# A bidirectional mLSTM and delta-rule layer on one core: when the decay loads, four modulation sums and the first z pieces are issued, and how the hand-over from output projection to FFN is cut

## The chip, the core and the metric

The kernel runs on one core of a Trainium2 chip. The metric is device time in microseconds (us) of one execution. The engines that matter are TensorE (PE, matrix products and transposes), VectorE (DVE), ScalarE (ACT), GpSimd (POOL, here it clears small tiles, scales a few blocks and issues small transfers) and SyncE (SP, it issues the weight loads).

## The reference

One layer on 256 tokens of width 2048, all in float32:

```python
mod = silu(c) @ ada_w + ada_b           # shift, scale, gate of the mixer and of the FFN
h = rms_norm(x) * (1 + scale_m) + shift_m
proj = h @ w_in                         # columns of branch A, branch B and the merge gates
y_a = (sigmoid(a_o) * norm(bidirectional(mlstm, q_a, k_a, v_a))) @ w_branch_a      # 4 heads
y_b = (norm(bidirectional(gated_delta, q_b, k_b, v_b)) * silu(b_z)) @ w_branch_b   # 16 heads
x = x + gate_m * ((g_a * y_a + g_b * y_b) @ w_out)
hf = rms_norm(x) * (1 + scale_f) + shift_f
gt, up = split(hf @ w_gate_up)          # 5632 columns each
x = x + gate_f * ((silu(gt) * up) @ w_down)
return rms_norm(x)
```

The gated delta rule works in chunks of 64 tokens; every chunk inverts a unit triangular matrix (`triangular_solve`), whose entries hold products of keys, beta and ratios of the decay.

## The kernel before

**Products in three parts.** A float32 weight block is loaded (`raw_*`, 1 MB), rounded on ScalarE to its high part (`wh_*`) and subtracted on VectorE to its low part (`wl_*`); the activations have a high and a low part too (`hh`/`hl`, later `mgh`/`mgl` and `hfh`/`hfl`). PE then multiplies high by high (L229), high weight by low activation (L230) and low weight by high activation (L231). `tjob` does this for 512 output columns and both halves of the tokens (`t`), in halves of a block: 12 matmuls of 512 columns for each `wh`/`wl` pair. There are three `raw` buffers and three of `wh` and of `wl`.

**Order.** Helper generators hand out pieces of such products ("jobs") between the steps of the recurrent branches, and `pump` adds from time to time one sum of the modulation (`ada_parts`, L111: a load of 1 MB and one VectorE instruction over 128x2048 that multiplies and accumulates). `every[0]` sets after how many job pieces a sum comes. The four engines' programs are otherwise put in order by a scheduler; instructions wrapped in `order(...)` keep the order of the code among themselves.

**Branch B.** Its 16 heads run in four groups. `gdn_phase1(h)` prepares a head: the decay factors `al` come from HBM, broadcast to all partitions (`decay_load`, 256 KB), four scans (L586 to L589) make `dec` of them, PE makes the key and query products `ks`, ten VectorE instructions (L633 to L642) and a transpose make the triangular blocks `mi` and `mb` (one buffer each). POOL stores `mi` to HBM in four transfers (`inst_d`, L649) and loads the blocks back into the layout of the inversion (`uu`, L652). `gdn_invert(g)` inverts the blocks of the group's four heads on VectorE, `gdn_phase2` applies them. `corners` copies blocks of `mi` and `mb` to `cc` on ScalarE; it is put off until the next `settle()`. Between two groups stands the job `z` (`z_job`, the output gate of the next group).

**Output projection and FFN.** `o` is made in four column blocks (`o0` to `o3`). For `o3` the last four row blocks are done first for token half 0 and then for token half 1 (`by_token`), so that the end of half 0 overlaps PE's work on half 1. For each half, `residual` multiplies by the gate (`tmss`, L1166), adds to `x` (L1167) and takes the sum of squares on ScalarE (L1170); `token_rstd` sums the four parts, takes the root and the reciprocal (L1178 to L1180). Then `normed` scales the token rows (`xn`), `moved` transposes a block of 128 features on PE (`pxn`), scales and shifts it (`hf`, L1264 or L1262), rounds it to `hfh` (L1265), and `low` makes `hfl` (L1268). The first FFN column block `gt0` runs beside that, in pairs of feature blocks. `d` (the down projection) ends like `o3`, with `finish` in place of the transposes.

Of the kernel before, what the change touches and what calls it, by code (L numbers as in the profile page):

```python
# [9 lines left out]
F32 = mybir.dt.float32  # L10
# [42 lines left out]
def hybrid_block(ctx: ExitStack, tc: tile.TileContext, xr, nfr, crow, pk_d, cst_d, ada2, ada4, win0, winb, wint, wba, wbb, wo, wgu, wd, out, dbg=None):  # L53
# [138 lines left out]
                done(o)  # L192
            yield True

    def tjob(name, chunks, xh, xl, done, early=0, by_token=None, steps=1):

        raws = {}  # L200

        def halves(u, k0):
            if u not in raws:
                raws[u] = raw_tile([P, 4, 512], f"raw_{name}_{u}")
                nc.sync.dma_start(raws[u], chunks[u])
            wh = st.tile([P, 2, 512], F32R, tag="wh", bufs=3, name=f"wh_{name}_{u}_{k0}")
            wl = st.tile([P, 2, 512], F32R, tag="wl", bufs=3, name=f"wl_{name}_{u}_{k0}")
            order(S.activation(wh, raws[u][:, k0 : k0 + 2], AF.Copy), early)  # L208
            settle()
            order(V.tensor_tensor(wl, raws[u][:, k0 : k0 + 2], wh.bitcast(F32), ALU.subtract), early)  # L210
# [12 lines left out]
        for n, (u, k0) in enumerate(todo):  # L223
            wh, wl = made.pop(0) if made else halves(u, k0)
            for k in range(2):
                kk = 4 * u + k0 + k
                for t in range(2):
                    c = slice(t * P, (t + 1) * P)
                    order(PE.matmul(ps[t], xh[:, kk, c], wh[:, k], start=kk == 0, stop=False), early and steps > 1)  # L229
                    PE.matmul(ps[t], xl[:, kk, c], wh[:, k], start=False, stop=False)  # L230
                    PE.matmul(ps[t], xh[:, kk, c], wl[:, k], start=False, stop=kk == last)  # L231
            if k0:
                pump()
                if u == len(chunks) - 1:
                    done(ps)
            yield True
            if early and steps > 1:
                if n + early < len(todo):
                    made.append(halves(*todo[n + early]))
                yield True  # L240
        if by_token:
            w = [halves(len(chunks) - 1, k0) for k0 in (0, 2)]
            by_token()
            for t in range(2):
                c = slice(t * P, (t + 1) * P)
                for k in range(4):
                    kk = last - 3 + k
                    wh, wl = (a[:, k % 2] for a in w[k // 2])
                    PE.matmul(ps[t], xh[:, kk, c], wh, start=False, stop=False)
                    PE.matmul(ps[t], xl[:, kk, c], wh, start=False, stop=False)  # L250
                    PE.matmul(ps[t], xh[:, kk, c], wl, start=False, stop=kk == last)
                done(t, ps[t])
                yield True

    def run(job):
# [323 lines left out]
    def gdn_phase1(h):  # L579
# [9 lines left out]
        V.tensor_tensor_scan(  # L589
            dec[:, 1, 256:384][:, ::-1], ab[:, 0:P][:, ::-1], ident[:, ::-1], 0.0, ALU.mult, ALU.add  # L590
        )
        if h + 2 < NH_B:
            decay_load(h + 2)

        sq = fr.tile([P, 2, T], F32, tag="sqkq", bufs=1, name=f"sqkq{h}")
        S.activation(sq, kq, AF.Square)
# [49 lines left out]
            uus[g] = bk.tile([64, 32, 32], F32, tag="uu", bufs=1, name=f"uu{g}")  # L646
        inst = inst_d[g][16 * hl_ : 16 * hl_ + 16]
        for b in range(4):
            G.dma_start(  # L649
                inst[4 * b : 4 * b + 4].rearrange("x j i -> j x i"), mi[32 * b : 32 * b + 32, :, 32 * b : 32 * b + 32]  # L650
            )
        G.dma_start(uus[g][16 * hl_ : 16 * hl_ + 16], inst)  # L652

        cc = ccs[h % NB]

# [350 lines left out]
    for g in range(4):  # L1006
# [6 lines left out]
        if g == 3:  # L1013
# [146 lines left out]
    gm = wp.tile([P, D], F32, name="gm")  # L1160
    row(2, gm, wp)

    def residual(t, g, ps, gate, ss, rp, hold=False, between=None):
        c = slice(g * 512, (g + 1) * 512)
        tm = rp.tile([P, 512], F32, tag="tm", bufs=2, name=f"tm{ss.name}_{t}_{g}")
        order(V.tensor_tensor(tm, ps, gate[:, c], ALU.mult), hold)  # L1166
        order(V.tensor_tensor(x1[:, t, c], x1[:, t, c], tm, ALU.add), hold)  # L1167
        if between:
            between()
        order(S.activation(tm, x1[:, t, c], AF.Square, accum_out=ss[:, t, g : g + 1]), hold)  # L1170

    def root():

        order(S.activation(rs1[:, 2:3], ones1, AF.Sqrt))

    def token_rstd(ss, rs, t):
        r = rs[:, t : t + 1]
        order(V.tensor_reduce(r, ss[:, t], mybir.AxisListType.X, ALU.add))  # L1178
        order(S.activation(r, r, AF.Sqrt, bias=epsc, scale=1.0 / D))
        order(V.reciprocal(r, r))  # L1180

    ss1 = xp.tile([P, 2, 4], F32, name="ss1")
    rs1 = xp.tile([P, 3], F32, name="rs1")
    sgs, later, xns, hfs = {}, {}, {}, {}

    class Late:
# [17 lines left out]

    gt0 = gate(0)
    affn = xp.tile([P, KB], F32, name="affn")
    for g in range(4):
        def done_o(*a, g=g):
            for t, ps in [a] if g == 3 else enumerate(a[0]):
                residual(t, g, ps, gm, ss1, wp, g == 3, None if g < 3 or t else lambda: next(gt0))  # L1210
                if g == 3:
                    token_rstd(ss1, rs1, t)

        if g == 3:
            root()
        front = (lambda: None) if g == 3 else None
        for i, _ in enumerate(tjob(f"o{g}", [wo[g, u] for u in range(4)], mgh, mgl, done_o, by_token=front)):
# [13 lines left out]
    sc.close()  # L1231
    pool(ctx, "edgeF").tile([P, 56], F32, name="edgeF")
    fp = pool(ctx, "fp")
    sh = ExitStack()
    hp = pool(sh, "hp", side="right")
# [6 lines left out]
    def normed(q, t, parts, eng):  # L1242
        if q not in xns:
            xns[q] = hp.tile([P, 2, 512], F32, tag="sg", bufs=2, name=f"xn{q}")
        o, i = xns[q][:, t, parts], x1[:, t, q * 512 + parts.start : q * 512 + parts.stop]
        if eng is G:
            G.tensor_scalar(o, i, rs1[:, t : t + 1], None, ALU.mult)
        elif eng is V:
            order(V.tensor_scalar(o, i, rs1[:, t : t + 1], None, ALU.mult))
        else:  # L1250
            order(S.activation(o, i, AF.Copy, scale=rs1[:, t : t + 1]))

    def moved(b):

        px = gps(f"pxn{b}")
        for t in range(2):
# [1 line left out]
            order(PE.transpose(px[:, t * P : (t + 1) * P], xns[b // 4][:, t, f : f + P], ident))  # L1258
        hfs[b] = hp.tile([P, T], F32, tag="hf", bufs=2, name=f"hf{b}")
        f, m = affn[:, b : b + 1], mod[:, 3 * KB + b : 3 * KB + b + 1]  # L1260
        if b % 2 and b > 2:
            order(S.activation(hfs[b], px[:, 0:T], AF.Identity, scale=f, bias=m))  # L1262
        else:
            order(V.tensor_scalar(hfs[b], px[:, 0:T], f, m, ALU.mult, ALU.add))  # L1264
        order(S.activation(hfh[:, b], hfs[b], AF.Copy))  # L1265

    def low(b):
        order(V.tensor_tensor(hfl[:, b], hfs.pop(b), hfh[:, b].bitcast(F32), ALU.subtract))  # L1268

    normed(0, 0, slice(0, 256), S)  # L1270
    normed(0, 1, slice(0, 256), V)
    for t in range(2):
        normed(0, t, slice(256, 512), S)
    moved(0)
    moved(1)
    low(0)
    moved(2)
    low(1)
    next(gt0)
    moved(3)  # L1280
    for t in range(2):
        normed(1, t, slice(0, 512), G)
    for b in range(2, KB, 2):

        next(gt0)
        low(b)
        low(b + 1)
        next(gt0)
        for e in (b + 2, b + 3):
            if e < KB:  # L1290
                moved(e)
# [25 lines left out]
    sums(P)  # L1317
    row(5, gf, dp)
    ss2 = xp.tile([P, 2, 4], F32, name="ss2")
    rs2 = xp.tile([P, 2], F32, name="rs2")  # L1320

    def finish(t):

        token_rstd(ss2, rs2, t)
        r = rs2[:, t : t + 1]
        for g in (2, 0, 3, 1):
            o = x1[:, t, g * 512 : (g + 1) * 512]
# [6 lines left out]
        for g in (2, 0, 3, 1):  # L1334
            c = slice(g * 512, (g + 1) * 512)
            order(nc.sync.dma_start(out[:, t, c], x1[:, t, c]))

    for g in range(4):
        c = slice(g * 512, (g + 1) * 512)

        def done_d(*a, g=g):
            for t, ps in [a] if g == 3 else enumerate(a[0]):
                residual(t, g, ps, gf, ss2, dp, g == 3)
                if g == 3:
                    finish(t)

        run(tjob(f"d{g}", [wd[g, u] for u in range(KD)], ffh, ffl, done_d, by_token=root if g == 3 else None))
# [104 lines left out]
```

## Time and profile before

| | |
|---|---|
| three runs | 2069.92, 2070.02 and 2065.7 us (median 2069.92) |
| the profiled execution | 2071.1 us, of it 2069.3 us from the first to the last instruction |
| mean granted TensorE clock | 0.992 |
| busy: PE, VectorE, ScalarE, POOL | 2022.9, 1395.8, 1026.0, 116.3 us |
| loads and stores | 485.64 MB, 235 GB/s on average |

A line of a list of waits names who waited, on which line and for what, then the microseconds in total, how often, and the longest. A line of a timeline has the start, the length, the engine, the line, the operation and its tiles, and in brackets how long the engine had been idle before it and what ended that. A line of a table of windows has for each engine the busy time in that stretch, then the granted clock (1.00 is full speed), the share of the transfer engines and GB/s. `x3` behind a row means three instructions told as one.

### The profile page before, as it was taken

The numbers are of one execution on the slowest core, as the hardware profiler recorded it, in microseconds if no ns is written. First come the engines' busy times: TensorE is split into PE (matmuls) and PEld (weight loads), VectorE is DVE, ScalarE is ACT, GpSimd is POOL, SyncE is SP. The second block draws the span as 40 slices with busy tenths as digits, with TensorE's granted clock in tenths as the row PEclk, the third lists the DMA queues.
The fourth block names the chain that finished last, engine by engine and source line by source line (L and its number), as shares of the span: only waits on it lengthen the run. The fifth ranks groups of instructions, "written<-read, shape, count | busy, mean of one in ns | idle before, by whom it ended". The sixth has DMA issues, their size and how long they took to land.

```text
span 2069.3 us, 26993 instructions
## 1 busy us (share of the span) xinstructions
PE 2022.9 (98%) x10374; PEld 1698.4 (82%) x10374; DVE 1395.8 (67%) x2059; ACT 1026.0 (50%) x1538; POOL 116.3 (6%) x211
## 2 busy tenths in 40 slices
PE   9999999999999999999999999999999999999997
PEld 7878779988997898889777778788888888878886
DVE  5778686777888788766577877555565654455554
ACT  3146546765675677465534434544444444444443
POOL 0001210111011011200100000100000000000000
PEclk9999999999999999999999999999999999999999
DMA  9986666546666765686867976366766665555553
GB/s 400 420 333 210 164 214 204 174 158 212 222 217 228 245 216 202 225 307 220 295 234 303 365 305 233 135 243 226 256 231 224 247 238 186 187 200 192 194 193 133
DMA packets 78962, 485.64 MB, mean 235 GB/s; under 512 B 10585, under 2 KB 15969, under 8 KB 24433
## 3 DMA queue, kind: packets, MB, share of 16 engines
q1 hardware_dynamic: 63360, 450.95, 60.3%
q0 software_dynamic: 8160, 17.88, 3.9%
q10 hardware_dynamic: 7314, 15.10, 1.9%
q8 instruction: 81, 1.33, 0.3%
q14 instruction: 47, 0.39, 0.1%
HBM read 467.07 MB, written 16.82 MB: 234 GB/s over the span
## 4 chain that ended last, share of the span: by engine, by line
PE 78%; DVE 5%; DMA 3%; ACT 2%; issue 1%; POOL 0%; ACTq 0%; DVEq 0%; SPq 0%
PE acc_up L231 4%; PE acc_up L230 4%; PE acc_up L229 4%; PE acc_d L231 4%; PE acc_d L230 4%; PE acc_d L229 4%; PE acc_gt L229 4%; PE acc_gt L230 4%; PE acc_gt L231 4%; PE acc_o L231 3%; PE acc_o L229 3%; PE acc_o L230 3%; PE acc_b L187 2%; PE acc_b L188 2%; PE acc_b L189 2%; PE acc_mb L231 1%
## 5 line engine op out<-in xcount | busy, mean ns | idle before, releaser
L210 DVE TENSOR_TENSOR wl_d<-raw_d,wh_d 128x1024 fp32r<-128x1024 f32 x88 | 107.8, 1225 | 119.9 <-ACT wh_d L208 119.9
L210 DVE TENSOR_TENSOR wl_up<-raw_up,wh_up 128x1024 fp32r<-128x1024 f32 x88 | 107.6, 1225 | 110.2 <-ACT wh_up L208 110.2
L210 DVE TENSOR_TENSOR wl_gt<-raw_gt,wh_gt 128x1024 fp32r<-128x1024 f32 x88 | 107.8, 1225 | 90.3 <-ACT wh_gt L208 90.3
L187 PE MATMUL acc_b<-hh,wh_b 128*128 128x256 f32 x576 | 164.6, 286 | 0.1
L208 ACT ACTIVATE wh_d<-raw_d 128x1024 fp32r<-128x1024 f32 x88 | 93.3, 1061 | 139.0 <-PE acc_d L230 134.0
L189 PE MATMUL acc_b<-hh,wl_b 128*128 128x256 f32 x576 | 160.7, 279 | 0.0
L188 PE MATMUL acc_b<-hl,wh_b 128*128 128x256 f32 x576 | 159.6, 277 | 0.0
L208 ACT ACTIVATE wh_gt<-raw_gt 128x1024 fp32r<-128x1024 f32 x88 | 93.3, 1060 | 128.7 <-PE acc_gt L230 77.2
L111 DVE SCALAR_TENSOR_TENSOR ada<-ada,crow 128x2048 f32<-128x2048 f32 x64 | 146.2, 2284 | 12.7 <-DMA ada<-ada 12.5
L208 ACT ACTIVATE wh_up<-raw_up 128x1024 fp32r<-128x1024 f32 x88 | 93.2, 1060 | 116.4 <-PE acc_up L230 82.9
L229 PE MATMUL acc_gt<-wh_gt,hfh 128*128 128x512 f32 x352 | 139.7, 397 | 0.9 <-ACT hfh L1265 0.9
L230 PE MATMUL acc_gt<-wh_gt,hfl 128*128 128x512 f32 x352 | 138.9, 395 | 0.0
L231 PE MATMUL acc_gt<-wl_gt,hfh 128*128 128x512 f32 x352 | 138.0, 392 | 0.0
L229 PE MATMUL acc_up<-wh_up,hfh 128*128 128x512 f32 x352 | 136.9, 389 | 0.0
L230 PE MATMUL acc_up<-wh_up,hfl 128*128 128x512 f32 x352 | 136.9, 389 | 0.0
L231 PE MATMUL acc_up<-wl_up,hfh 128*128 128x512 f32 x352 | 136.8, 389 | 0.0
L229 PE MATMUL acc_d<-wh_d,ffh 128*128 128x512 f32 x344 | 134.3, 391 | 0.0
L230 PE MATMUL acc_d<-wh_d,ffl 128*128 128x512 f32 x344 | 134.3, 390 | 0.0
L231 PE MATMUL acc_d<-wl_d,ffh 128*128 128x512 f32 x344 | 133.9, 389 | 0.0
L553 PE MATMUL first<-x,raw 128*128 128x256 f32 x512 | 115.9, 386 | 5.5 <-ACT x L547 5.4
L553 PEld LDWEIGHTS first<-x,raw 128*128 128x128 f32 x512 | 97.3, 192 | 24.2 <-ACT x L547 11.2
L208 ACT ACTIVATE wh_o<-raw_o 128x1024 fp32r<-128x1024 f32 x64 | 67.8, 1060 | 88.9 <-PE acc_o L230 65.8
(370 smaller groups left out, 5293.2 us busy)
## 6 DMA issues: line engine op xcount, KB each, us to landing
ada<-ada SPq DMA_DIRECT2D x64, 1024.0 KB, 5.2
raw_gt<-wgu SPq DMA_DIRECT2D x44, 1024.0 KB, 5.0
raw_up<-wgu SPq DMA_DIRECT2D x44, 1024.0 KB, 4.9
raw_d<-wd SPq DMA_DIRECT2D x44, 1024.0 KB, 4.9
raw_b<-winb SPq DMA_DIRECT2D x36, 1024.0 KB, 5.0
ra<-ada SPq DMA_DIRECT2D x32, 1025.0 KB, 15.1
raw<-win SPq DMA_DIRECT2D x16, 1024.0 KB, 14.5
raw_z<-wint SPq DMA_DIRECT2D x16, 1024.0 KB, 5.1
```

The costliest lines, as they stand in the source:

```text
L111: V.scalar_tensor_tensor(raw, raw, 1.0, row_c[:, :D], ALU.mult, ALU.mult, accum_out=mod[:, c : c + 1])
L187: PE.matmul(o, wh[:, k], hh[:, kk], start=kk == 0, stop=False)
L188: PE.matmul(o, wh[:, k], hl[:, kk], start=False, stop=False)
L189: PE.matmul(o, wl[:, k], hh[:, kk], start=False, stop=kk == KB - 1)
L208: order(S.activation(wh, raws[u][:, k0 : k0 + 2], AF.Copy), early)
L210: order(V.tensor_tensor(wl, raws[u][:, k0 : k0 + 2], wh.bitcast(F32), ALU.subtract), early)
L229: order(PE.matmul(ps[t], xh[:, kk, c], wh[:, k], start=kk == 0, stop=False), early and steps > 1)
L230: PE.matmul(ps[t], xl[:, kk, c], wh[:, k], start=False, stop=False)
L231: PE.matmul(ps[t], xh[:, kk, c], wl[:, k], start=False, stop=kk == last)
L553: PE.matmul(first[o], raw[:, o], x[:, b], start=b == 0 and o % 2 == 0, stop=b == KB - 1 and o % 2 == 1)
```

## The change

Six things are changed. (1) In `gdn_phase1` the load of the decay of head `h + 2` moves from behind the scans of head `h` to behind the four stores of its `mi`; the stores and the `uu` load keep the order of the code. (2) `every[0]` is 4 in the first group where it was 0, so four of the modulation sums are made there; the sums behind them all move up by four. (3) The `z` job of the next group is set up one step earlier, ahead of the last step of the group's second pair, with its first half block prepared and its instructions kept in the order of the code. (4) `o3`'s last four row blocks are done for token half 0, then for the left 256 columns of half 1, then for the right 256 columns, in a third accumulator. The sums of squares of the first three column blocks are added up ahead of time (`means`), and the root takes them as its bias (`token_root`). (5) For the even blocks, and for blocks 1, `hfh` is made by ScalarE straight from the transposed block in PSUM, beside `hf` on VectorE. (6) The end of `d` uses `means` and `token_root` too.

```diff
 gdn_phase1:
-        if h + 2 < NH_B:
-            decay_load(h + 2)
...
         for b in range(4):
-            G.dma_start(
+            order(G.dma_start(
                 inst[4 * b : 4 * b + 4].rearrange("x j i -> j x i"), mi[32 * b : 32 * b + 32, :, 32 * b : 32 * b + 32]
-            )
-        G.dma_start(uus[g][16 * hl_ : 16 * hl_ + 16], inst)
+            ), b)
+
+        if h + 2 < NH_B:
+            decay_load(h + 2)
+        order(G.dma_start(uus[g][16 * hl_ : 16 * hl_ + 16], inst))
 the groups of branch B:
-        every[0] = (0, 2, 2, 2)[g]
+        every[0] = (4, 2, 2, 2)[g]
...
+                if n == 9 and p and g < 3:
+
+                    zj = z_job(g + 1, int(4 * g + 7 in heads))
+                    if 4 * g + 7 in heads:
+                        next(zj)
                 next(pairs[p], None)
...
-            fills.insert(0, z_job(g + 1))
+            fills.insert(0, zj)
 tjob, by_token:
-            for t in range(2):
+            for i, (t, part) in enumerate(parts):
+                if i > 1:
+                    ps.append(acc_ps.tile([P, 512], F32, tag="acc", name=f"acc_{name}_{i}"))
                 c = slice(t * P, (t + 1) * P)
+                o = ps[i][:, : part.stop - part.start]
                 for k in range(4):
                     kk = last - 3 + k
-                    wh, wl = (a[:, k % 2] for a in w[k // 2])
+                    wh, wl = (a[:, k % 2, part] for a in w[k // 2])
...
+    def means(ss, rs):
+
+        order(V.tensor_reduce(rs[:, 3:5], ss[:, :, 0:3], mybir.AxisListType.X, ALU.add))
+        order(V.tensor_scalar(rs[:, 3:5], rs[:, 3:5], 1.0 / D, EPS, ALU.mult, ALU.add))
+
+    def token_root(rs, t):
+
+        order(S.activation(rs[:, t : t + 1], rs[:, 5 + t : 6 + t], AF.Sqrt, bias=rs[:, 3 + t : 4 + t], scale=1.0 / D))
...
+    def last_o(t, ps, part):
+
+        sq = rs1[:, 5 + t : 6 + t]
+        if not t:
+            residual(0, 3, ps, gm, ss1, wp, True, acc=sq)
+            token_root(rs1, 0)
+        elif part == left:
+            residual(1, 3, ps, gm, ss1, wp, True, acc=sq, new=left)
+            order(V.scalar_tensor_tensor(rs1[:, 4:5], sq, 1.0 / D, rs1[:, 4:5], ALU.mult, ALU.add))
+            token_rstd(rs1, 0)
+            normed(0, 0, left, S)
+        else:
+            residual(1, 3, ps, gm, ss1, wp, True, part, sq, part)
+            token_root(rs1, 1)
+            token_rstd(rs1, 1)
+
+    def front_o():
+        next(gt0)
+        means(ss1, rs1)
 block (before: moved):
-        order(S.activation(hfh[:, b], hfs[b], AF.Copy))
+        def high():
+            if b % 2 and b > 2:
+                order(S.activation(hfh[:, b], hfs[b], AF.Copy))
+            else:
+                order(S.activation(hfh[:, b], px[:, 0:T], AF.Identity, scale=f, bias=m))
```

POOL's program at heads 0 and 1 before. `al` is a decay load, `inst_d<-mi` a store of a triangle, `uu` the load back; the first two rows fetch the decay of head 2, the next such pair that of head 3.

```order
L308 MEMSET al_1182 128x2x8
L309 DMA al_1182<-alpha_d 128x2x256
L649 DMA inst_d_118<-mi_1271 32x4x32 x3
L308 MEMSET al_1199 128x2x8
L309 DMA al_1199<-alpha_d 128x2x256
L649 DMA inst_d_118<-mi_1271 32x4x32
L652 DMA uu_1290<-inst_d_118 16x1024
L649 DMA inst_d_118<-mi_1312 32x4x32 x4
L652 DMA uu_1290<-inst_d_118 16x1024
```

And now:

```order
L651 DMA inst_d_118<-mi_1265 32x4x32 x4
L312 MEMSET al_1289 128x2x8
L313 DMA al_1289<-alpha_d 128x2x256
L657 DMA uu_1284<-inst_d_118 16x1024
L651 DMA inst_d_118<-mi_1309 32x4x32 x4
L312 MEMSET al_1332 128x2x8
L313 DMA al_1332<-alpha_d 128x2x256
L657 DMA uu_1284<-inst_d_118 16x1024
```

Head 0's fourth store stood behind a decay load; now all four stores of a head stand ahead of it, and the `uu` load stands behind it. Heads 2 and 3 are moved in the same way.

VectorE's program at the turn from the first group to the second before: head 7's triangle (`mi`, `mb`, `gg`, `at` out of `ks`) and the low parts of job `z`.

```order
L210 TENSOR_TENSOR wl_z_0_2_3753<-raw_z_0_3728,wh_z_0_2_3752 128x1024
L210 TENSOR_TENSOR wl_z_1_0_3771<-raw_z_1_3768,wh_z_1_0_3770 128x1024
L633 SCALAR_TENSOR_TENSOR mi_3691<-ks_0_3695,sm_3681,dec_3630 128x128
L634 SCALAR_TENSOR_TENSOR mb_3692<-ks_0_3695,sm_3681,dec_3630 128x128
L636 TENSOR_TENSOR gg_3693<-ks_0_3695,dec_3630 128x128
```

And now, from the last rows of the triangle on:

```order
L644 TENSOR_TENSOR at_3703<-ks_1_3711,dec_3641 128x256
L645 STREAM_TRANSPOSE mi_3700<-mb_3701 128x256
L211 TENSOR_TENSOR wl_z_0_0_3730<-raw_z_0_3727,wh_z_0_0_3729 128x1024
L590 SCALAR_TENSOR_TENSOR dec_4611<-al_3487,cst 128x256
L591 SCALAR_TENSOR_TENSOR dec_4611<-al_3487,cst 128x128
L592 SCALAR_TENSOR_TENSOR dec_4611<-al_3487,cst 128x256
L211 TENSOR_TENSOR wl_z_0_2_3765<-raw_z_0_3727,wh_z_0_2_3764 128x1024
L211 TENSOR_TENSOR wl_z_1_0_3783<-raw_z_1_3780,wh_z_1_0_3782 128x1024
```

Three low parts of `z` stood ahead of the triangle (the first, `wl_z_0_0`, stood eight rows above the triangle); now all stand behind it.

ScalarE's program at the same turn, now. `obt` is the output of the group's last pair, `cc` the corners of head 7.

```order
L209 ACTIVATE wh_z_0_0_3729<-raw_z_0_3727 128x1024
L830 ACTIVATE obt_3743<-px_1_3594,pk 128x256
L830 ACTIVATE obt_3746<-px_1_3594,pk 128x256
L664 ACTIVATE cc_1161<-mi_3700 32x2x32
L831 DMA ob_d_114<-obt_3743 128x256
L664 ACTIVATE cc_1161<-mb_3701 32x2x32
L664 ACTIVATE cc_1161<-mi_3700 32x2x32
L664 ACTIVATE cc_1161<-mb_3701 32x2x32
L667 ACTIVATE cc_1161<-mi_3700 64x2x64
L667 ACTIVATE cc_1161<-mb_3701 64x2x64
L831 DMA ob_d_114<-obt_3746 128x256
L209 ACTIVATE wh_z_0_2_3764<-raw_z_0_3727 128x1024
```

Before, `wh_z_0_2` and `wh_z_1_0` stood ahead of the two `obt` and the six `cc`; now the second high part of `z` stands behind all of them.

More of the change, by code (lines that the diff above doesn't have):

```diff
@@ L193, in fjob, with tjob @@
             yield True
[L195 removed]
+    def tjob(name, chunks, xh, xl, done, early=0, by_token=None, steps=1, parts=((0, slice(0, 512)), (1, slice(0, 512)))):
         raws = {}
@@ L1240, in hybrid_block, with block @@
     ffl = fp.tile([P, FB, T], F32R, name="ffl")
[L1242 to L1253, printed above, removed]
+    def block(b):
         px = gps(f"pxn{b}")
@@ L1260, in moved, with scaled, pair @@
         f, m = affn[:, b : b + 1], mod[:, 3 * KB + b : 3 * KB + b + 1]
[L1261 to L1265, printed above, removed]
+        def scaled():
+            if b % 2 and b > 2:
+                order(S.activation(hfs[b], px[:, 0:T], AF.Identity, scale=f, bias=m))
+            else:
+                order(V.tensor_scalar(hfs[b], px[:, 0:T], f, m, ALU.mult, ALU.add))
+        def high():
+            if b % 2 and b > 2:
+                order(S.activation(hfh[:, b], hfs[b], AF.Copy))
+            else:
+                order(S.activation(hfh[:, b], px[:, 0:T], AF.Identity, scale=f, bias=m))
+        return scaled, high
     def low(b):
         order(V.tensor_tensor(hfl[:, b], hfs.pop(b), hfh[:, b].bitcast(F32), ALU.subtract))
-    normed(0, 0, slice(0, 256), S)
-    normed(0, 1, slice(0, 256), V)
-    for t in range(2):
-        normed(0, t, slice(256, 512), S)
-    moved(0)
-    moved(1)
+    def pair(b, split):
+        (s0, h0), (s1, h1) = block(b), block(b + 1)
+        s0()
+        split()
+        h0()
+        s1()
+        h1()
+        low(b)
+        low(b + 1)
+    normed(0, 1, left, V)
+    for t in range(2):
+        normed(0, t, right, S)
+    for b in range(2):
+        scaled, high = block(b)
+        scaled()
+        high()
     low(0)
-    moved(2)
     low(1)
-    next(gt0)
-    moved(3)
+    pair(2, lambda: next(gt0))
     for t in range(2):
@@ L1285, in hybrid_block @@
         next(gt0)
[L1286 to L1291, printed above, removed]
+        if b + 2 < KB:
+            pair(b + 2, lambda: next(gt0))
+        else:
+            next(gt0)
         if b % 4 == 0 and b < 12:
@@ L1341, in done_d @@
         def done_d(*a, g=g):
[L1342 to L1347, printed above, removed]
+            if g == 3:
+                residual(a[0], g, a[1], gf, ss2, dp, True, acc=rs2[:, 5 + a[0] : 6 + a[0]])
+                finish(a[0])
+            else:
+                for t, ps in enumerate(a[0]):
+                    residual(t, g, ps, gf, ss2, dp)
+        run(tjob(f"d{g}", [wd[g, u] for u in range(KD)], ffh, ffl, done_d, by_token=front_d if g == 3 else None))
         if g < 3:
```

67 lines of the change are left out of this document (39 added, 28 removed).

## Prediction

> **What bounds the kernel now.** I read the page first, for the busiest engine:
>
> ```profile
> span 2069.3 us, 26993 instructions
> PE 2022.9 (98%) x10374; PEld 1698.4 (82%) x10374; DVE 1395.8 (67%) x2059; ACT 1026.0 (50%) x1538; POOL 116.3 (6%) x211
> ```
>
> PE is busy for 98% of the span, and the change takes no product away from it (column halves are twice as many matmuls of half the width). So the change can only win or lose in PE's waits and in PE's clock. The list of PE's waits, the rows that the change touches:
>
> ```profile
> PE acc_v L231 <- DVE wl_v L210: 7.0, 3, 4.8
> ...
> PE pxn L1258 <- ACT xn L1251: 3.6, 1, 3.6
> PE acc_o L231 <- DVE wl_o L210: 2.7, 1, 2.7
> ...
> PE acc_z L229 <- ACT wh_z L208: 2.5, 1, 2.5
> PE p L775 <- DVE pt L764: 1.5, 1, 1.5
> PE vps L599 <- ACT vf L333: 1.4, 1, 1.4
> ...
> PE acc_gt L229 <- ACT hfh L1265: 0.9, 3, 0.3
> ```
>
> Then the table of windows, for the granted clock (the 0.50, 0.51 and 1.00 behind POOL's time):
>
> ```profile
> 257.80:261.20 3.40, 0.07 (x1) 0.08 (x1) 3.40 (x11) 2.41 (x7) 1.46 (x3) 1.00 0.08 22
> 261.20:264.60 3.40, 3.40 (x8) 2.67 (x9) 3.40 (x5) 1.23 (x2) 1.23 (x3) 0.50 0.77 231
> ...
> 824.40:827.80 3.40, 3.40 (x10) 2.63 (x9) 2.36 (x2) 2.59 (x3) 0.53 (x2) 0.50 0.25 43
> 1315.90:1322.80 6.90, 6.33 (x19) 5.02 (x20) 4.83 (x11) 5.31 (x11) 4.83 (x3) 0.51 0.01 2
> ```
>
> Behind a long wait PE works for 3.4 us (once 6.9) at half rate, which costs 1.7 us for each 3.4. The Trainium skill, "TensorE: Matmul & The Clock Gate", section "What's actually happening", says why this need not repeat: the monitor's window of 3413 ns runs free of the kernel's start. No run here shows two profiles of one kernel, so I leave every drop where it was unless its wait goes.
>
> **Part 1, decay loads behind the stores.** POOL's and VectorE's timeline, and one row of PE's:
>
> ```profile
> 208.01 1.67 POOL L649 DMA_DIRECT2D inst_d<-mi  x3 [12.13 <-DVE mi L643]
> ...
> 220.52 2.17 POOL L649 DMA_DIRECT2D inst_d<-mi  x4 [2.24 <-DVE mi L643]
> 227.17 0.51 POOL L652 DMA_DIRECT2D uu<-inst_d  x1 [4.48 <-DMA inst_d<-mi]
> ...
> 245.57 1.64 POOL L649 DMA_DIRECT2D inst_d<-mi  x3 [14.08 <-DVE mi L643]
> ...
> 247.66 0.72 POOL L309 DMA_DIRECT2D al<-alpha_d  x1 [0.32 <-issue]
> 248.36 0.57 POOL L649 DMA_DIRECT2D inst_d<-mi  x1
> ```
> ```profile
> 217.29 0.35 DVE L633 SCALAR_TENSOR_TENSOR mi<-ks,sm,dec 128x128 f32<-128x128 f32 x1 [3.44 <-DMA inst_d<-mi]
> ...
> 257.04 0.35 DVE L633 SCALAR_TENSOR_TENSOR mi<-ks,sm,dec 128x128 f32<-128x128 f32 x1 [7.27 <-DMA inst_d<-mi]
> ...
> 259.89 2.32 DVE L210 TENSOR_TENSOR wl_v<-raw_v,wh_v 128x1024 fp32r<-128x1024 f32 x2
> ```
> ```profile
> 221.38 0.50 PE L231 MATMUL acc_v<-wl_v,hh 128*128 128x512 f32 x1 [0.99 <-DVE wl_v L210]
> 261.12 0.73 PE L231 MATMUL acc_v<-wl_v,hh 128*128 128x512 f32 x1 [4.78 <-DVE wl_v L210]
> ```
>
> `mi` has one buffer, so head 3's triangle waits for head 2's last store, which stands behind a decay load: issued at 248.36, it is over at 257.0, 8.6 later. Without a decay load between (head 1), 6.65 pass from the first store's issue to the moment all have landed (220.52 to 227.17). So head 3's triangle can start at 245.57 + 6.65 = 252.2 instead of 257.04. It takes 2.9 (257.04 to 259.89), `wl_v` another 1.2, so that is there at 256.3. PE asks for it at 256.3 (261.12 less its wait). That wait goes, 4.8, and with it the half-rate window behind it, 1.7. What is late next is `wl_v`'s neighbour, just in time; I take off 0.1. In the pair of heads 0 and 1, the other two waits (2.3 together), head 1's triangle gets 208.0 + 6.65 = 214.7 instead of 217.29. But one `wl_v` that VectorE made during that wait now stands behind the triangle: it comes at 214.7 + 2.9 + 1.2 = 218.8, and PE wants it one half block (2.7, below) ahead of the next, at 221.38 - 0.99 - 2.7 = 217.7. A new wait of 1.1 and one like it behind the convolutions make up for the two, so I count this pair as zero. Part 1: **-6.4** (bounds: -8.7 when the first pair's waits go too, -2 when the stores still take as long as they did).
>
> The `uu` load now stands behind the decay load (the timeline, and the table of transfers, whose last number is the median from issue to landing):
>
> ```profile
> 456.65 0.52 POOL L652 DMA_DIRECT2D uu<-inst_d  x1 [1.74 <-DMA inst_d<-mi]
> ...
> 460.96 0.16 DVE L684 TENSOR_TENSOR utmp<-uu 64x30 f32<-64x30 f32 x1 [0.96 <-issue]
> ```
> ```profile
> al<-alpha_d POOLq DMA_DIRECT2D x16, 256.0 KB, 7.0
> ```
>
> The load takes 4.3 from issue to VectorE's first step of the inversion, and VectorE's stream waits there, with `z`'s third `wl_z` now a few rows behind it. PE wants that `wl_z` at 449.4 + 4 x 2.75 + 3.0 + 0.46 = 463.9 (`z`'s start, four half blocks, part 3's delay there, two matmuls), and VectorE has some eight short steps (an estimate of 2.1, from 0.16 for the first, growing) and 1.2 ahead of it: `uu` has to be there by 460.6. Issued at 455.7, as the triangle ends 1 us earlier (part 3), it would be, at 460.0; with the decay load ahead of it, issued at some 454.3 and 7.0 long, it is there at 461.5 or so. I take **+1.0** for the three turns together (0 to 15: a rival).
>
> **Part 2, four sums in the first group.** Each is one row on VectorE:
>
> ```profile
> L111 DVE SCALAR_TENSOR_TENSOR ada<-ada,crow 128x2048 f32<-128x2048 f32 x64 | 146.2, 2284 | 12.7 <-DMA ada<-ada 12.5
> ```
>
> In the second group eight of them go with two waits of PE, 1.5 and 1.4 (`p` and `vps` above), which puts a sum at up to 0.36; in the other groups less, so 0.15 each: **+0.6** (0 to 4, if each delays a `wl` by most of its 2.28). They leave `o0` and `o1`, where PE has no wait but the one of 2.7 at `o0`'s start. That one waits for a sum whose load is issued where it was, so it stays.
>
> **Part 3, z's first pieces earlier.** The turn from the first group to the second, where PE has no wait today:
>
> ```profile
> 447.31 1.88 PE L628 MATMUL ks<-kq 128*128 128x512 f32 x4
> ...
> 449.51 0.34 DVE L633 SCALAR_TENSOR_TENSOR mi<-ks,sm,dec 128x128 f32<-128x128 f32 x1
> ```
> ```profile
> L231 PE MATMUL acc_z<-wl_z,hh x30: 388/388/388, 449.9 to 469.8; 128*128 128x512 f32 x30
> ```
>
> The last row gives PE's step: 87 matmuls in 19.9 us, 0.229 each, with `z` from 449.4 on. VectorE now makes the triangle first and the first `wl_z` behind it. The triangle needs `ks`, over between 448.4 (first half) and 449.2, and takes 2.9; so the `wl_z` is there at 452.5 or later. PE runs four matmuls that don't need it, to 450.3, and waits 2.2. The second `wh_z` now stands behind six corner copies, which need the finished triangle:
>
> ```profile
> 635.85 1.06 ACT L208 ACTIVATE wh_z<-raw_z 128x1024 fp32r<-128x1024 f32 x1
> ...
> 639.93 0.26 ACT L659 ACTIVATE cc<-mi 32x64 f32<-32x64 f32 x1 [0.53 <-DVE wl_z L210]
> ...
> 641.65 1.06 ACT L208 ACTIVATE wh_z<-raw_z 128x1024 fp32r<-128x1024 f32 x1
> ```
>
> That is the second turn. 1.7 of copies (639.93 to 641.65), 1.06 of `wh_z`, 1.2 of `wl_z`: to be set against the 1.8 that PE still has of the first half block and the two matmuls that it can run ahead: some 0.8 more. So +3.0 at the first turn. At the second the first pieces stand as they did, but the second `wh_z` (before at 635.85, in time) comes behind copies and two `obt`: +2.0. At the third the wait of 2.5 goes, since `wh_z` no longer waits for `obt`, and with it the half-rate window at 824.4 (1.7), but waits for the first `wl_z`, the second `wh_z` and its `wl_z` of 1.8, 1.4 and 0.8 come in: zero. Part 3: **+5.0** (-4, if the first two turns are covered by other work, to +8).
>
> **Parts 4 and 5, from o to the FFN.** VectorE and PE, then ScalarE:
>
> ```profile
> 1313.25 0.67 DVE L1166 TENSOR_TENSOR tmss<-acc_o,gm 128x512 f32<-128x512 f32 x1
> ...
> 1316.25 0.35 DVE L1249 TENSOR_SCALAR xn<-x,rs 128x256 f32<-128x256 f32 x1
> ```
> ```profile
> 1316.47 0.90 PE L1258 MATMUL pxn<-cst,xn 128*128 128x128 f32 x3 [3.60 <-ACT xn L1251]
> ```
> ```profile
> 1324.35 0.42 ACT L1265 ACTIVATE hfh<-hf 128x256 fp32r<-128x256 f32 x1 [1.74 <-DVE hf L1264]
> ...
> 1328.37 0.42 ACT L1265 ACTIVATE hfh<-hf 128x256 fp32r<-128x256 f32 x1 [1.75 <-DVE hf L1264]
> ```
>
> PE ends `o3` when it did, at 1312.9 (1316.47 less the wait). Of half 1 the left columns are there 1.4 earlier, at 1311.5; VectorE's two rows on them (0.67 each and a hand-over), ScalarE's squares and half 0's reciprocal fill it to about 1314.2, and only then the right `tmss` starts, 0.95 later than now but half as wide in each of its steps: `xn` of half 1 at about 1316.2, as before. What is saved is `hfh` no longer waiting for `hf`: PE's first `gt0` matmul comes 0.75 earlier. In `gt0` ScalarE and VectorE pass a pair of blocks to and fro in 4.02 (1324.35 to 1328.37), where PE needs 12 x 0.229 and four transposes (0.22 each at half rate in the row of 1316.47, so 0.11), 3.2. Without the step from `hf` to `hfh` on each other's heels ScalarE has one `wh` of 1.06 and three passes of 0.4 to 0.6 for a pair, an estimate of under 2.9. PE loses between the 0.9 of its wait row and 3 x 0.8 by it now; I take 1.8. Of the two half-rate windows from 1315.9 the second may go, as `gt0` starts earlier: 1.7, taken at a half. **-3.4** (-1 to -6, the end with both windows gone).
>
> **Part 6, the end of d.** One row and its hand-over go from each half:
>
> ```profile
> 2058.33 0.16 DVE L1178 TENSOR_REDUCE rs<-ss 128x1 f32<-128x4 f32 x1 [0.79 <-ACT tmss L1170]
> ```
>
> 0.2 each, **-0.4**.
>
> **The sum.** -6.4 + 1.0 + 0.6 + 5.0 - 3.4 - 0.4 = -3.6. The profiled execution took 2071.1 (its span and 1.8 around it) and would take 2067.5. It lies 1.2 above the median of the runs, 2069.92, so I forecast 2066.3, rounded to **2066**.
>
> **Rivals.** (a) *The first turns are covered*: VectorE and ScalarE reach `z`'s pieces early enough, and part 3 is worth 0 instead of 5.0: 2061.3. For it: before, the third turn lost 2.5 and a window. Against it: the order of the rows, in which `wl_z` stands behind `ks`.
> (b) *The stores stay slow*: the 8.6 at 248.36 came from weight loads and not from the decay load; part 1 is worth 2: 2070.7. Against it: the 6.65 of head 1's four stores, in the same stretch of weight loads.
> (c) *Slower: the `uu` load inherits the wait.* What made the fourth store take 8.6 was its place behind a decay load; now `uu` has that place. Issued at 455.7, plus 8.6, it lands at 464.3, 3.7 later than VectorE can stand (460.6), and the `wl_z` behind the inversion's first steps is late by as much, at each of three turns, with a half-rate window behind two of them: 3 x 3.7 + 2 x 1.7, less the 1.0 counted, is 13.5 more: 2079.8. It decides where `uu` lands past 460.6. Against it: `uu` is issued only when the stores have landed, and the decay load is nearly through by then. The Trainium skill, "DMA: Bandwidth & Descriptors", section "Two DMAs through the same engine are not ordered", says that descriptors of one queue start in order; by that the `uu` load waits until the decay load's have started, which speaks for (c). The trace agrees in the 8.6 at 248.36.
>
> **The numbers.** My forecast 0.55, (a) 0.17, (b) 0.13, (c) 0.15. The forecast's own terms spread by some 3 us (the clock's windows and the bounds above). About 0.2%, 4.1 us, is what a measurement can tell from no change: faster is below 2065.8, slower above 2074.1. Of the forecast's 0.55, 0.28 is faster and 0.27 the same; (a) is faster; (b) the same but for 0.03; (c) slower. Faster 0.48, same 0.37, slower 0.15. The range, 3 us to either side of (a) and 2 above (b), leaves out (c) and little else: 2058 to 2073.
>
> **What would show it.** Right: the wait of 4.8 for `wl_v` is gone, and the clock at 261 is 1.00; new waits of PE for `wl_z` at the first two turns, 2 to 3 each; none for `hfh` in `gt0`. Wrong: no `wl_z` wait at the first turn (then a), `mi` still waiting over 3 for `inst_d` (b), VectorE waiting over 3 for `uu` (c).

## The result, and the profile after

The changed kernel is slower: 2074.36 us (median of 20 runs, 2067.97 to 2078.92) against 2068.91 (20 runs, 2065.7 to 2073.54). The ratio is 1.0022, its 95% interval 1.0015 to 1.0029, so the change costs 3.1 to 6.0 us. The forecast of 2066 and its range, up to 2073, are both missed. The profiled execution took 2068.26 and is one of the fastest of the twenty, so its waits are read below, and not its time. A second profiled execution of the same kernel (`again`) took 7.6 us more, 4.4 of it between 560 and 600, and has more half-rate windows (9 against 6).

The page after, first rows, and PE's waits, in the rows that answer those of before:

```profile
span 2066.3 us, 27021 instructions
PE 2018.8 (98%) x10386; PEld 1693.9 (82%) x10386; DVE 1397.4 (68%) x2062; ACT 1027.5 (50%) x1540; POOL 115.6 (6%) x211
```
```profile
PE acc_z L232 <- DVE wl_z L211: 11.2, 10, 3.9
PE vps L601 <- ACT vf L337: 3.2, 3, 2.5
PE acc_o L232 <- DVE wl_o L211: 2.4, 1, 2.4
PE pxn L1298 <- DVE xn L1233: 1.8, 1, 1.8
PE acc_z L230 <- ACT wh_z L209: 1.7, 2, 0.9
PE pxn L1298 <- ACT xn L1235: 1.5, 1, 1.5
...
PE acc_v L232 <- DVE wl_v L211: 0.9, 1, 0.9
PE acc_gt L230 <- ACT hfh L1312: 0.6, 1, 0.6
```

The 7.0 of `acc_v` is 0.9, as part 1 wanted. In its place `acc_z` waits 11.2 for `wl_z`. Before it waited for that once, 1.1 at 148 us (the 11.2 has it too), and at no turn between groups:

```profile
PE acc_z L231 <- DVE wl_z L210: 1.1, 1, 1.1
```

PE's busy time is 4 us lower, and most of its other waits are nearly what they were.

Where `acc_z` waits, PE's, VectorE's and POOL's timelines at the turn from the first group to the second show:

```profile
444.46 0.73 PE L232 MATMUL acc_z<-wl_z,hh 128*128 128x512 f32 x2 [1.90 <-DVE wl_z L211]
...
459.47 0.50 PE L232 MATMUL acc_z<-wl_z,hh 128*128 128x512 f32 x1 [3.87 <-DVE wl_z L211]
```
```profile
440.38 0.35 DVE L635 SCALAR_TENSOR_TENSOR mi<-ks,sm,dec 128x128 f32<-128x128 f32 x1 [4.44 <-PE ks L630]
...
443.23 1.18 DVE L211 TENSOR_TENSOR wl_z<-raw_z,wh_z 128x1024 fp32r<-128x1024 f32 x1
...
456.26 0.16 DVE L689 TENSOR_TENSOR utmp<-uu 64x30 f32<-64x30 f32 x1 [6.62 <-issue]
...
458.21 1.21 DVE L211 TENSOR_TENSOR wl_z<-raw_z,wh_z 128x1024 fp32r<-128x1024 f32 x1
```
```profile
443.60 2.17 POOL L651 DMA_DIRECT2D inst_d<-mi  x4 [16.94 <-DVE mi L645]
...
445.81 0.73 POOL L313 DMA_DIRECT2D al<-alpha_d  x1
447.52 0.52 POOL L657 DMA_DIRECT2D uu<-inst_d  x1 [0.98 <-DMA inst_d<-mi]
```

Two waits came in. The 1.90 is the first `wl_z` (443.23) behind the triangle that starts at 440.38. The 3.87 is the fifth low part (the first of `z`'s third block): VectorE stood idle for 6.62, until the `uu` load was there, and made that `wl_z` only at 458.21. From the issue of the `uu` load (447.52) to the inversion's first step (456.26) pass 8.7, where before it was 4.3. Over all sixteen heads the table of transfers has 6.4 instead of 4.3 (after, then before; the last number is the median from issue to landing):

```profile
uu<-inst_d POOLq DMA_DIRECT2D x16, 64.0 KB, 6.4
```
```profile
uu<-inst_d POOLq DMA_DIRECT2D x16, 64.0 KB, 4.3
```

The table of windows shows what a wait of that length brings with it, and that the wait at 261 has taken its window with it (the clock is the number ahead of the last two):

```profile
254.00:257.40 3.40, 3.40 (x17) 2.78 (x16) 2.49 (x5) 1.77 (x2) 0.16 (x1) 1.00 1.03 344
456.50:459.90 3.40, 0.43 (x2) 0.38 (x3) 3.16 (x10) 0.68 (x1) 0.00 (x0) 1.00 0.10 41
459.90:463.30 3.40, 3.40 (x10) 2.61 (x9) 3.19 (x9) 0.00 (x0) 0.00 (x0) 0.50 0.00 0
463.30:466.70 3.40, 3.40 (x17) 2.78 (x16) 3.23 (x8) 1.58 (x2) 0.00 (x0) 1.00 0.88 308
```

The Trainium skill, "TensorE: Matmul & The Clock Gate", section "What's actually happening", states that the clock drops after an idle window of about 3.4 us and returns after a busy one. The trace agrees here: 0.43 busy out of 3.40, then 3.40 at 0.50, then 1.00.

Lining up PE's matmuls of both traces one by one gives the account (us ahead of before is minus; worked out from the start of the same matmul in each):

| stretch of before | after | what |
|---|---|---|
| to 266 | -8.5 | `acc_v` no longer waits, first pair of heads 1.7 and second 6.6, its half-rate window in it |
| 266 to 445 | +0.5 | four sums |
| 445 to 470 | +8.3 | waits of 1.90 and 3.87, a half-rate window, small ones |
| 636 to 660 | +4.6 | second turn: five waits of 0.3 to 0.9, and small ones |
| 818 to 860 | +0.4 | third turn |
| 1060 to 1240 | -3.8 | before had 3.4 at half rate at 1066 and 6.8 at 1230, this execution only 3.4 at 1231 |
| 1300 to 1370 | -1.3 | from `o` to the FFN |

The stretches between make -2.5 together, none of them more than 1, so this execution ends up 2.2 ahead at the last matmuls. The timed runs are 4.6 behind: single executions can differ by as much.

### The profile page after: what moved, and what is told of

Read it like the earlier page. It is cut to its first block, busy times and chain, and to the rows that moved or that the text cites. A ratio compares the mean times of both kernels' runs of the same rounds, so it can differ in the third digit from the quotient of the medians.

```text
span 2066.3 us, 27021 instructions
## 1 busy us (share of the span) xinstructions
PE 2018.8 (98%) x10386; PEld 1693.9 (82%) x10386; DVE 1397.4 (68%) x2062; ACT 1027.5 (50%) x1540; POOL 115.6 (6%) x211
## 4 chain that ended last, share of the span: by engine, by line
PE 86%; DVE 5%; DMA 5%; ACT 1%; issue 1%; POOL 0%; ACTq 0%; SPq 0%; DVEq 0%; POOLq 0%
PE acc_gt L230 4%; PE acc_gt L231 4%; PE acc_gt L232 4%; PE acc_up L230 4%; PE acc_up L231 4%; PE acc_up L232 4%; PE acc_d L232 4%; PE acc_d L231 4%; PE acc_d L230 4%; DMA ra<-ada 3%; PE acc_o L232 3%; PE acc_o L230 3%; PE acc_o L231 3%; PE acc_b L187 3%; PE acc_b L189 3%; PE acc_b L188 3%
## 5 line engine op out<-in xcount | busy, mean ns | idle before, releaser
L209 ACT ACTIVATE wh_gt<-raw_gt 128x1024 fp32r<-128x1024 f32 x88 | 93.3, 1060 | 128.7 <-PE acc_gt L231 77.3
L209 ACT ACTIVATE wh_up<-raw_up 128x1024 fp32r<-128x1024 f32 x88 | 93.2, 1060 | 118.1 <-PE acc_up L231 84.2
L209 ACT ACTIVATE wh_o<-raw_o 128x1024 fp32r<-128x1024 f32 x64 | 67.8, 1060 | 87.1 <-PE acc_o L231 62.3
```

## The experiments

Three theories stood after this: the `uu` load waits behind the decay load, which is worth most of what part 1 won; `z`'s first pieces, taken a step earlier, come behind the triangle and the corners; or the sums of the first group do it. For the first there were two mechanisms, which later expectations call D and E: D, the order within POOL's queue; E, the transfer engines, which all queues share. Other letters in an expectation stand for the theory that its own words describe. Each run stands against the kernel before on the same chip.

**1. The same kernel once more.** No edit.

> The changed kernel once more, for a second profile. Theory A (new waits for z's low parts at the turns between groups, the longest behind the uu load): a slower execution loses more at the same places, above all at the first turn around 455 us. Theory B (only the clock): the same waits, with more half-rate windows. Either way the median is 2071 to 2077.

2075.85 us, ratio 1.0024 (1.0013 to 1.0035). The slowdown repeats. This slower execution loses 8.1 at the first turn, no more than the first profile did, so theory A's account of the slower execution does not hold. It loses the rest in a longer wait for `vf` (3.50 where the first profile has 2.52) and in more half-rate windows, which is nearer to B.

**2. Without part 3.** The job `z` is set up where it was before:

```diff
-                if n == 9 and p and g < 3:
-                    zj = z_job(g + 1, int(4 * g + 7 in heads))
-                    if 4 * g + 7 in heads:
-                        next(zj)
...
-            fills.insert(0, zj)
+            fills.insert(0, z_job(g + 1))
```

> The changed kernel with part 3 undone: job z is set up after the group's pairs again, as in the kernel before. Theory A: the waits for wl_z at the three turns go (8.2, 3.4 and 0.5 us in the changed kernel's profile), so 2062 to 2066. Theory B: within 2 us of the changed kernel, 2072 to 2076. Theory C (the decay load ahead of the uu load is what costs, wherever z stands): about half of the loss stays, 2068 to 2070.

2068.02, ratio 0.9986 (0.9975 to 0.9997): 7.8 below the first run. Taking `z` early is a loss here. The time is what C has; A had 2062 to 2066. In the trace the turns still cost with `z` late: 3.4 at the first and 4.9 at the second, where PE waits 3.31 for a `wl_z`.

**3. The `uu` load ahead of the decay load**, part 3 kept:

```diff
+        order(G.dma_start(uus[g][16 * hl_ : 16 * hl_ + 16], inst))
         if h + 2 < NH_B:
             decay_load(h + 2)
-        order(G.dma_start(uus[g][16 * hl_ : 16 * hl_ + 16], inst))
```

> The changed kernel with the uu load put ahead of the decay load, directly behind the stores; z early as in the change. Theory A with z's order alone: the wait at 455 us shrinks but the first wl_z still waits 1.9 us for the triangle: 2070 to 2073. Theory C: most of the loss goes, 2064 to 2068. Theory B: no change.

2069.62, ratio 0.9991 (0.9979 to 1.0002): 6.2 below the first run, between the ranges of A and C. At the first turn POOL and VectorE now read

```profile
450.74 0.52 POOL L655 DMA_DIRECT2D uu<-inst_d  x1 [1.74 <-DMA inst_d<-mi]
...
451.30 0.73 POOL L313 DMA_DIRECT2D al<-alpha_d  x1
```
```profile
456.06 0.20 DVE L689 TENSOR_TENSOR utmp<-uu 64x30 f32<-64x30 f32 x1 [3.22 <-DMA uu<-inst_d]
```

5.3 from issue to first step instead of 8.7, and the wait of 3.87 is gone. The first wait, for the triangle, stays (1.91).

**4. Both.**

> Both undone: z set up late and the uu load ahead of the decay load; the decay loads still behind the stores. Theory A: like z_late, within 1 us, since with z late no low part of z stands behind the uu load: 2062 to 2066. Theory C: better than z_late by 3 or more.

2060.38, ratio 0.9948 (0.9933 to 0.9963), 15.5 below the first run, where the two edits have 14.0 between them. So the late `uu` load and the early `z` both cost, and nearly add up; neither lives off the other. C had it (3 or more below run 2, measured 7.6), A did not. In this trace PE waits 2 us for `vf` at 410, where the kernel before has no wait; a sum stands near by, hence the next runs.

**5. Decay loads on SyncE's queue.** The whole change, but from head 2 on the decay load is issued by SyncE:

```diff
-        order(G.dma_start(al[:, :, 8:], alpha_d[:, h].partition_broadcast(P)))
+        order((nc.sync if h > 1 else G).dma_start(al[:, :, 8:], alpha_d[:, h].partition_broadcast(P)))
```

> The changed kernel with the decay loads of heads 2 to 15 issued by SyncE into the queue of the weight loads, at the same place of the code. Theory D (the uu load is late because it stands in POOL's queue behind the decay load): the uu load takes 4 to 5 us to VectorE's first step at the first turn instead of 8.7, the wait at 455 us shrinks below 1, and the time is 2068 to 2071. Theory E (a decay load slows every transfer beside it, whatever queue it stands in): the uu load still takes 7 to 9 and the time stays 2073 to 2077; weight loads behind a decay load are late as well.

2069.47, ratio 1.000 (0.999 to 1.001). The time is what D has, but the trace does not bear D out. SyncE issues the decay load at another moment: for the first turn at 432.36, some 21 ahead of the `uu` load, which so has nothing in front of it (5.5 from its issue at 453.53 to the first step). Where a decay load and small transfers do meet, at head 0, POOL and SyncE read

```profile
207.88 2.25 POOL L651 DMA_DIRECT2D inst_d<-mi  x4 [12.91 <-DVE mi L645]
...
217.33 0.53 POOL L657 DMA_DIRECT2D uu<-inst_d  x1 [7.09 <-DMA inst_d<-mi]
```
```profile
209.44 0.38 SPq L313 DMA_DIRECT2D al<-alpha_d  x1
```

and here POOL's rows of the same place before:

```profile
208.01 1.67 POOL L649 DMA_DIRECT2D inst_d<-mi  x3 [12.13 <-DVE mi L643]
...
217.75 0.52 POOL L652 DMA_DIRECT2D uu<-inst_d  x1 [6.42 <-issue]
```

From the first store's issue to the issue of `uu` pass 9.45 with the decay load on another queue, and 9.74 with it on their own queue, between the third and the fourth store. In the changed kernel, with the decay load behind all four, it is 3.7 (207.84 to 211.54 on POOL). At head 2 it is 8.7 with the decay load on SyncE's queue (248.13 to 256.81), 12.3 before (245.57 to 257.85) and 3.9 in the changed kernel (243.73 to 247.67). So the order within one queue is not needed to hold a small transfer up: a decay load that started first does it from either queue, though at head 2 by less from the other. PE's waits for `wl_v` are back in this trace (5.2 in total, 0.9 in the changed kernel), and it is only 2.2 ahead of before at 266, where the changed kernel is 8.5. That they share the transfer engines (E) is what fits; no run shows where in the transfer the time goes. The Trainium skill, "DMA: Bandwidth & Descriptors", section "Queues, rings and completion order", says that each transfer engine takes its queues in turn, packet by packet; by that another queue's load can delay a store too, as it does here. It names no length for the delay.

**6 and 7. Best versions without the sums.** Both are kernel 4 with `every[0]` back at 0 in the first group; the second puts `uu` ahead of the decay load only in the last head of each group, where the inversion waits for it:

```diff
-        every[0] = (4, 2, 2, 2)[g]
+        every[0] = (0, 2, 2, 2)[g]
...
+        if hl_ == GRP - 1:
+            order(G.dma_start(uus[g][16 * hl_ : 16 * hl_ + 16], inst))
         if h + 2 < NH_B:
             decay_load(h + 2)
-        order(G.dma_start(uus[g][16 * hl_ : 16 * hl_ + 16], inst))
+        if hl_ < GRP - 1:
+            order(G.dma_start(uus[g][16 * hl_ : 16 * hl_ + 16], inst))
```

> z late, the uu load ahead of the decay load, and no sums in the first group (part 2 undone as well). In the profile with the sums, PE waits 2.0 us at 410 for vf, with a half-rate window behind it. If the sums cause that wait: 2 to 5 us better than z_late_uu_first's 2060.4, so 2055 to 2059. If they cost only the 0.6 of the prediction: 2059 to 2061.

> As no_sums_best, but the uu load goes ahead of the decay load only in the last head of each group, the one that the inversion waits for; in the other three heads the decay load goes first as in the change. Theory A/C: the first pair's waits shrink as in the changed kernel (1.6 us better than uu_first at 230 us) and nothing else changes: 1 to 2 better than no_sums_best. If a decay load that starts earlier slows the weight loads of its time (562 us), that takes the gain back: 0 to 3 worse.

2062.38, ratio 0.9966 (0.9955 to 0.9978), and 2059.97, ratio 0.9954 (0.9942 to 0.9967). Neither can be told from kernel 4, and the first missed both ranges of its expectation (2055 to 2059 and 2059 to 2061). The wait at 410 is in neither trace, but nothing is won by that in time: the theory of the sums falls.

**8. The tail alone**: parts 4, 5 and 6 on the kernel before.

> The kernel before with parts 4, 5 and 6 alone (o3 by column halves, hfh straight from PSUM, the ends of o and d). By the prediction's terms 3.8 us faster than before; by the two profiles, in which PE's lead grew by 1.3 from 1300 to 1370 us, 1 to 3.

2066.15, ratio 0.9984 (0.9975 to 0.9993): -3.3 (-5.2 to -1.4). In its trace PE gains 2.6 between `o` and the FFN, and 0.4 goes from the stretch behind the last matmul (10.5 before, 10.1 now).

**9. Part 1 alone**, with the `uu` load behind the decay load; nothing else of the change.

> Part 1 alone: decay loads behind the stores and the uu load behind the decay load; no sums, z as before, tail as before. If the queue order is the cause (theory D), part 1's 8 us are almost given back by the late uu load, which was worth 7.6 with z late: within 3 us of the kernel before. If part 1 is worth 8 and the uu load costs 1, as the prediction has it, 5 to 7 us faster than before.

2069.38, ratio 1.0004 (0.9996 to 1.0013): +0.8 (-0.8 to +2.7). Its trace is 8.3 ahead at 266, as the whole change was, and 1.4 ahead at 660. The rows show three places that gave it back: VectorE's first step of the inversion and PE behind it, and the next group's values, with the window that follows:

```profile
455.71 0.16 DVE L685 TENSOR_TENSOR utmp<-uu 64x30 f32<-64x30 f32 x1 [4.03 <-issue]
...
462.51 1.21 DVE L210 TENSOR_TENSOR wl_mb<-raw_mb,wh_mb 128x1024 fp32r<-128x1024 f32 x1
```
```profile
471.24 0.51 PE L231 MATMUL acc_mb<-wl_mb,hh 128*128 128x512 f32 x1 [1.69 <-DVE wl_mb L210]
```
```profile
560.91 0.44 PE L597 MATMUL vps<-cst,vf 128*128 128x128 f32 x2 [3.03 <-ACT vf L333]
```
```profile
562.10:565.50 3.40, 3.40 (x18) 3.40 (x18) 2.97 (x14) 1.56 (x4) 0.00 (x0) 0.51 0.39 164
```

With `z` where it was, the late `uu` load (448.33 to 455.71, 7.4) falls on the job behind `z`: 2.4 from 445 to 490 by the lined-up matmuls. The wait for `vf`, 1.44 before, is 3.03 and brings a half-rate window: 3.1. At the second turn two waits for `wl_z`, 1.06 and 1.16, make 2.2. Together 7.7 of part 1's 8.3, of which 0.8 came back in between. (The execution ends 5.4 ahead, mostly because it misses the window that before had at 1066 and half of the one at 1230; the timed runs do not show that gain.)

**10. Part 3 alone.**

> Part 3 alone: z's first pieces a step earlier, the rest as before, so the uu load is not behind a decay load. If z early costs what the two differences of the first runs say (7.8 and 9.2), 6 to 10 us slower than before. If it costs what the prediction has for it, 5 us slower; if its cost came only from meeting the late uu load, 0 to 3 slower.

2075.6, ratio 1.0033 (1.0021 to 1.0046): +6.8 (+4.3 to +9.5). Its first turn has the same first wait, with the `uu` load near its old speed (5.2 from issue to first step, 4.3 before):

```profile
452.90 0.74 PE L231 MATMUL acc_z<-wl_z,hh 128*128 128x512 f32 x2 [1.90 <-DVE wl_z L210]
```

**11. The best order with the sums**: kernel 7 with `every[0]` at 4.

> The whole change without part 3, with the uu load ahead of the decay load in the last head of a group only and behind it in the others, and with the four sums in the first group. By the best two so far 2058 to 2062; if the sums make PE wait in the first group (the 2 us at 410 of the run with uu first and z late) 2 to 5 more than the same kernel without sums, if they save as much later, the same.

2059.2, ratio 0.9958 (0.9946 to 0.997): the sums are worth nothing either way that the times show. The wait for `vf` at 410 is back in this trace (1.56), and the kernel is no slower than kernel 7. Of the waits followed here little of `wl_z` is left (1.1 of the 1.3 is at 148, as before); what is left is the wait for `vf`:

```profile
PE vps L601 <- ACT vf L337: 5.7, 4, 3.7
...
PE acc_z L230 <- ACT wh_z L209: 2.5, 1, 2.5
...
PE acc_z L232 <- DVE wl_z L211: 1.3, 2, 1.1
```

Kernels 4, 6, 7 and 11, which leave part 3 out and let `uu` go first where it is waited for, beat both the kernel before and the changed one, by 7 to 11 us against before.

## Why the prediction was wrong, step by step

| step | predicted | measured |
|---|---|---|
| part 1 without the `uu` load | -6.4 | -8.3 (trace) |
| `uu` load behind the decay load | +1.0 | +6 to +9 (runs 3, 4 and 9) |
| part 1 as it was made | -5.4 | +0.8 (-0.8 to +2.7) |
| sums | +0.6 | +0.5 (trace, 266 to 445); none that the times show |
| part 3 | +5.0 | +6.8 (+4.3 to +9.5) |
| parts 4 to 6 | -3.8 | -3.3 (-5.2 to -1.4) |
| sum | -3.6 | 0.8 + 6.8 - 3.3 = +4.3; the whole change +4.6 (3.1 to 6.0) |

**The step that failed** is "with the decay load ahead of it, issued at some 454.3 and 7.0 long, it is there at 461.5 or so. I take +1.0". It lets the `uu` load land with the decay load, as if its own transfer took no time. In the trace the two come one after the other: from the decay load's issue (445.81) to VectorE's first step (456.26) pass 10.4, near the 7.0 and the 4.3 of the two rows that stood in the prediction. Their sum, 11.3, put behind 454.3, gives 465.6, and would have called for rival (c). (c) said 3.7 late with a half-rate window behind it; the first turn has 3.87 and the window. It expected that at three turns. The second had waits of 0.3 to 0.9 only (with `z` late, in run 2's trace, one of 3.31 and a window), and at the third no decay load is left to be fetched, since `h + 2` is past the last head; the wait for `vf` and the window at 560, which I had no step for, came instead.

The step failed in a second way. It asked only whether `z`'s `wl_z` would be late. Run 9 shows that with `z` out of the way the same lateness is paid by `wl_mb`, by `vf` and at the second turn: 7.7, nearly all that part 1 had won.

**Part 3** was right in sign and place and undersized by 1.8, within the interval of run 10. Of the first turn's 4.4 in run 10's trace, 2.5 is the predicted wait (2.2 was the estimate, 1.90 the row). The 0.8 for the second `wh_z` did not come; 1.9 came at four later low parts, from 461 to 470, which I left out. The second turn had 1.8 where I had 2.0, the third 0.4 where I had zero.

**Part 1's mechanism** was right: the stores land in time and the wait of 4.8 and its window are gone. They land even sooner than I said: head 2's are through 3.9 after the first issue, where I took 6.65 from head 1, and head 1's still take 7.0. I had counted the first pair of heads as zero; it gave 1.7.

**Parts 4 to 6** came out as summed, though the half window (0.85) that I counted did not come: 6.8 us from 1315.9 ran at half rate before, and 6.8 from 1312.6 in run 8. In `gt0` a pair of feature blocks now takes 3.21, where it took 4.02 and PE's own work was put at 3.2. ScalarE's timeline:

```profile
1327.38 0.57 ACT L1312 ACTIVATE hfh<-pxn,mod,affn 128x256 fp32r<-128x256 f32 x1 [0.88 <-DVE hf L1306]
...
1330.59 0.57 ACT L1312 ACTIVATE hfh<-pxn,mod,affn 128x256 fp32r<-128x256 f32 x1 [0.78 <-DVE hf L1306]
```

**What stays open.** Why `vf` is late at 560 the traces show in part. On ScalarE `vf` stands behind `wh_a`, which waits for a weight load of 1 MB (`raw_a`). Before, and then run 9 (the first bracket names another transfer, but `raw_a` landed at 563.9, 5.0 after its issue):

```profile
563.96 1.06 ACT L182 ACTIVATE wh_a<-raw_a 128x1024 fp32r<-128x1024 f32 x1 [2.81 <-DMA kq_d<-ev_a]
565.10 0.42 ACT L333 ACTIVATE vf<-cv 128x256 f32<-128x256 f32 x1
```
```profile
559.49 1.06 ACT L182 ACTIVATE wh_a<-raw_a 128x1024 fp32r<-128x1024 f32 x1 [4.59 <-DMA raw_a<-winb]
560.46 0.40 ACT L333 ACTIVATE vf<-cv 128x256 f32<-128x256 f32 x1
```

In six of the thirteen traces the decay load of this place is issued 3.3 to 3.6 ahead of that weight load. There the weight load takes 6.0 to 7.5 from issue to landing, and PE waits 2.5 to 3.7 for `vf`. In the other seven it is issued behind, the weight load takes 5.0 to 5.4 (one has no landing on record), and PE waits 1.4 to 1.9. Three pairs of kernels differ here in nothing but the order of the decay load and the `uu` load: the changed kernel and run 3, runs 2 and 4, runs 7 and 6. So the decay load slows the weight load too, by some 1 to 2. What that is worth in time stays open: run 7, which has the longer wait, is no slower than run 6. Kernel 11 has the wait in spite of its order in the last heads, since 560 belongs to a first head, where its decay load still goes first.

## What to carry to other kernels

A transfer that is moved behind another has to be priced with both lengths in series, 7.0 + 4.3 here, and not with the later of the two ends. When a load is taken out of one critical transfer's way, look whose way it now stands in: the decay load left the stores (8.3 won) and stood in front of the load back that the inversion waits for (6 to 9 lost); letting the waited-for load go first keeps the gain. And preparing a piece of work earlier is worth nothing where its engine's order puts it behind something that is itself late: `wl_z` went behind the triangle, and cost 6.8.

## What was not expected of the hardware

The decay load of 256 KB delays 16 KB stores from SyncE's queue too: at head 0 as much as from their own (9.45 and 9.74), at head 2 less (8.7 and 12.3).

The half-rate windows differ between executions of one kernel. The two profiled executions of the changed kernel had 6 and 9 of them and lay 7.6 us apart; six stand at the same places of the program, three only in the slower one. A busy PE does not rule them out:

```profile
989.00:992.40 3.40, 3.40 (x28) 3.26 (x28) 1.23 (x1) 1.06 (x1) 0.00 (x0) 1.00 0.90 305
992.40:995.80 3.40, 3.40 (x9) 2.65 (x9) 0.59 (x6) 0.24 (x2) 1.49 (x2) 0.50 0.44 141
```
```profile
989.07 2.73 PE L947 MATMUL pden<-ones,mdec 128*128 128x1 f32 x24
```

PE is busy here for all of the 3.40 us ahead of the half rate, but 2.73 of them are 24 matmuls of one column each. Every trace has two such rows, near 990 and 1065, and 14 of these 26 are followed by a half-rate window within 4 us, none, one or both in a trace. At 1.7 a window that is up to 3.4 us between two executions, at rows that the change does not touch. So a difference of a few us between single profiles need not be one in the timed runs: run 9 ended 5.4 ahead in its profile, and is 0.8 behind in time.
